# The last row block of three stages kept in SBUF for the next stage's operand

## The chip, the cores and the metric

The kernel runs on one core of a Trainium2 chip. The metric is the time of one execution in microseconds of the device; a kernel is run several times, and its time is the median. The engines of the core work side by side, each through its own row of instructions in a fixed order: TensorE (PE) multiplies, VectorE (DVE) and ScalarE (ACT) work on tiles in the on-chip memory (SBUF), GpSimd (POOL) and SyncE (SP) issue most of the transfers (DMAs) between SBUF and the memory of the chip. An instruction starts when the one ahead of it on its engine has, and when what it reads and the room that it writes are free.

## What is computed

One layer of a decoder, for 512 tokens of 2048 values in float32. Two branches (a spatial gating unit and an attention without softmax) give `y_a` and `y_b`; what matters here is what follows them:

```python
merged = sigmoid(g_a) * (y_a @ w_up_a) + sigmoid(g_b) * (y_b @ w_up_b)
x = x + merged @ w_o                                    # x1
h = rmsnorm(x, ffn_norm_g)
hid = h @ w_ffn_in
gate, up = hid[..., :FFN_HIDDEN], hid[..., FFN_HIDDEN:]
x = x + (silu(gate) * up) @ w_ffn_out                   # x2
ple = p @ w_ple
x = x + sigmoid(rmsnorm(x, ple_norm_g) @ w_ple_gate) * ple
```

## The kernel before

**Layout.** Activations are kept transposed: a block is 128 partitions by 1024 columns of float32, 512 KB, and holds 256 of the 2048 rows of x, of the merged rows or of x1 and x2 for all 512 tokens. So each of these has KU = 8 blocks, numbered 0 to 7. A product in float32 is made of products of shortened numbers: an operand is split into a high part (ScalarE, line 287 for activations and 367 for weights) and a low part (VectorE, lines 288 and 364), and TensorE adds high by high (L297), high by low weight (L299) and low by high (L298).

**Products.** A unit is the share that one row block of activations has in a pair of output blocks. It is taken plainly ("P": 12 products of 512 columns, L297 to L299) or by a scheme with seven products of half blocks in place of eight ("S", L703), which needs sums and differences of quarter blocks of the operand (L535) and of the weights (L383; some are added by GpSimd's transfers, L371). An S unit in the first output rows of a stage can still be run plainly: `HALF = 1, 1, 1, 1, 2, 2, 2, 2` and `FFN_UNTIL = 1, 1, 2, 2, 2, 2, 2, 2` say up to which output row each of the eight operands is used so. So an operand of kind S is made in two steps: first the plain parts, and later, before the first S product that needs them, the sums and differences. Both steps start from the raw block, which is loaded once for each (L526, by SP; `fetch` and `fetch_second`). At the gate the kinds are `GATE = "SSSSSSPP"`: the last two operands are plain and have one step.

**Two arenas in SBUF.** `parts` holds the operands; `wholes` has 13312 columns, room for 13 raw blocks of 1024, for everything else that is loaded or summed: raw blocks for operands, raw weights, output rows. A load waits until the block that it is given has been left by its last reader.

**What sets the order.** The program text is written once, in Python, and there is no order by hand. `tick()` runs once for each group of products. It moves on up to AHEAD = 3 of the operands in `builds`, the second steps in `seconds`, the weights planned ahead, and the functions in a waiting list: `after(n, fn)` runs `fn` n ticks later. An operand asks for room first; when `ready` says that its raw block is stored, `fetch` issues the load, and the split follows WAIT = 2 ticks later (`due`). So a change in when room is taken or given back moves later instructions on all engines.

**The stages around the change.** (1) For each of the 8 blocks j of merged rows, the two up-projections are multiplied by their gates and added (L1403); two ticks later `store` (L1376) writes the block to the chip's memory (L1377), marks it in `there` and gives its room back. The operands `ms` of w_o load it again. (2) w_o: each output is added onto the rows of x; the sum, x1, is written out (L1423), its squares go into the norm, and its room is given back. The operands `fs` of w_ffn_in load it again and scale it by the norm's gain (L530). (3) w_ffn_in, the hidden rows, which are written out and loaded back, and w_ffn_out in three chunks of the hidden rows; the first two chunks are added onto x1 in the chip's memory, the third onto a loaded x1, which gives x2 (L1481). Its operands `gs` at the gate load it again. The weights' loads (L340 plain; L342 and L350 for S) are on SP's queue as well, between all of these.

In all three places the block in question, j = 7, is the last that the stage before makes, and the first step of its operand is the last to be made.

Of the kernel before, what the change touches and what calls it, by code (L numbers as in the profile page):

```python
# [23 lines left out]
KU = D // (2 * P)  # L24
# [47 lines left out]
def hybrid_layer(  # L72
# [117 lines left out]
    clock = [0]  # L190
# [13 lines left out]
    def after(n, fn):  # L204
        heapq.heappush(waiting, (clock[0] + n, next(names), fn))
# [247 lines left out]
    class Form(Staged):  # L453
# [8 lines left out]

        def fetch(self):
            self.block, self.there, self.due = self.src(), True, clock[0] + WAIT
            self.sizes = self.sizes[:-1]

        def arrived(self):
# [905 lines left out]
            lambda size=1024: load(spill[n, j], size), lambda: (n, j) in there, gain, far=True,  # L1373
            **how)

    def store(n, j, block):  # L1376
        nc.sync.dma_start(out=spill[n, j], in_=block.f())  # L1377
        there.add((n, j))
        give(block)

    ms = [spilled_form("S", "mix", j) for j in range(KU)]
    build(ms)
    for j in range(KU):
        for b in "ab":
            s = load(gate_spill[b, j], 1024, "low")
            g = s.f()

            def gate(g=g):
                scaled(g, row1)
                nc.scalar.activation(g, g, AF.Sigmoid)  # L1390

            after(3, gate)
            pr = pair([ys[b, i] for i in range(4)], last=j == KU - 1, j=j,
                      until=(b == "b",) * 4)
            if pr.n["S"]:
                nc.vector.tensor_tensor(out=g, in0=g, in1=pr.o, op=ALU.mult)
            else:
                for h, ps in zip((g[:, :T], g[:, T:]), pr.ends()):
                    nc.vector.tensor_tensor(out=h, in0=h, in1=ps, op=ALU.mult)
            if b == "a":  # L1400
                part[j] = s
            else:
                nc.vector.tensor_tensor(out=g, in0=g, in1=part[j].f(), op=ALU.add)  # L1403
                give(part.pop(j))
                after(2, lambda j=j, s=s: store("mix", j, s))
        if not j:
            ple_operands()
        elif j < 6:
            ple_pair(j + 2)
            if j == 5:  # L1410
                ple_done()
# [5 lines left out]
    for j in range(KU):  # L1417
        h = load(xT[j])
        if j == 1:
            build(fs)  # L1420
        pr = pair(ms, last=j == KU - 1, j=j, until=HALF, doubled=7)
        pr.onto(h.f())
        nc.sync.dma_start(out=spill["x1", j], in_=h.f())  # L1423
        there.add(("x1", j))
        norm2.add(h)
        give(h)

# [33 lines left out]
    for c, units in enumerate(hs):  # L1463
# [3 lines left out]
        for j in range(KU):  # L1467
# [13 lines left out]
            nc.sync.dma_start(out=spill["x2", j], in_=h.f())  # L1481
            there.add(("x2", j))
            norm3.add(h)
            give(h)


    for j in range(KU):
# [130 lines left out]
```

## Time and profile before

| | |
|---|---|
| three runs | 2648.46, 2652.16, 2646.56 us; median 2648.46 |
| the profiled execution | 2647.41 us, of which the span of the profile is 2645.7 |
| granted clock of TensorE | 1.00 |
| busy: ScalarE, GpSimd | 54%, 17% of the span |
| read and written | 514.88 MB and 51.38 MB, 214 GB/s over the span |
| SP's queue (q1) | 444.70 MB, 51.3% of the time of 16 DMA engines |
| POOL's queue (q0) | 121.14 MB, 28.6% |

All times inside the execution are in us from the start of the span, and of one profiled execution; the span leaves out what lies around it, 1.7 us. A row of the timeline gives start, length, engine, line, operation, what it writes and reads, the shape, and how many like it follow one another; in brackets stands the idle time of the engine ahead of it with what ended it. SPq and DVEq are the parts of an engine that issue transfers and wait for them. TensorE overlaps its products, so the length of one is more than the distance between two.

### The profile page before, as it was taken

To read this page: it belongs to the slowest core of one execution; us is meant where nothing else is said; L and a number is where in the kernel's file an instruction comes from. 1 tells how busy PE (TensorE), PEld (TensorE's weight loads), DVE (VectorE), ACT (ScalarE), POOL (GpSimd) and SP (SyncE) were. 2 spreads that over 40 slices of the span, in tenths; PEclk is the share of its full clock that TensorE was granted. 3 is DMA by queue.
4 is the path that set the end of the run, shared out by engine and by line. 5 is a ranking of instruction groups with operands and counts; after the bars stand their busy time and mean duration, and the time that the engine had idled before them with its cause. 6 is when DMAs were issued, how large, how long until landed. Compare 5 with 4: busy or idle time off the path is not lost.

```text
span 2645.7 us, 43096 instructions
## 1 busy us (share of the span) xinstructions
PE 2631.0 (99%) x15454; PEld 2310.3 (87%) x15454; DVE 2300.3 (87%) x3953; ACT 1431.3 (54%) x2279; POOL 455.7 (17%) x573
## 2 busy tenths in 40 slices
PE   9999999999999999999999999999999999999999
PEld 7888888889998998888888888888888888889888
DVE  8687878787888779999888888888889989989898
ACT  7756565665555445465444444444445445455543
POOL 0222222232220001102111111111110211211010
PEclk9999999999999999999999999999999999999999
DMA  6777777777777879989988888788877989988884
GB/s 207 186 195 172 193 171 187 178 188 191 178 192 243 253 242 285 255 262 239 233 199 206 199 203 205 195 211 198 206 183 225 256 222 271 228 237 262 246 268 136
DMA packets 294533, 569.10 MB, mean 215 GB/s; under 512 B 26800, under 2 KB 137648, under 8 KB 294320
## 3 DMA queue, kind: packets, MB, share of 16 engines
q1 hardware_dynamic: 230240, 444.70, 51.3%
q0 software_dynamic: 63792, 121.14, 28.6%
q8 instruction: 121, 1.98, 0.3%
q14 instruction: 92, 0.75, 0.1%
q10 hardware_dynamic: 288, 0.52, 0.1%
HBM read 514.88 MB, written 51.38 MB: 214 GB/s over the span
## 4 chain that ended last, share of the span: by engine, by line
PE 91%; DVE 5%; DMA 2%; issue 1%; ACT 1%; SPq 0%; POOL 0%; DVEq 0%; ACTq 0%
PE ps L703 57%; PE ps L299 8%; PE ps L298 8%; PE ps L297 8%; PE small L703 6%; DVE wlo L364 1%; DVE parts L288 1%; DVE wholes L535 1%; PE small L1131 1%; PE small L1183 1%; PE small L1057 1%; DMA wholes<-hid 1%; DVE wholes L383 0%; PE small L1242 0%; ACT whi L367 0%
## 5 line engine op out<-in xcount | busy, mean ns | idle before, releaser
L703 PE MATMUL ps<-parts,whi 128*128 128x512 f32 x4390 | 1469.9, 398 | 0.1
L367 ACT ACTIVATE whi<-wholes 128x512 fp32r<-128x512 f32 (+2 forms) x948 | 883.5, 946 | 717.8 <-DVE wholes L383 324.3
L364 DVE TENSOR_TENSOR wlo<-wholes,whi 128x512 fp32r<-128x512 f32 (+2 forms) x948 | 993.3, 1083 | 40.4 <-ACT whi L367 39.9
L703 PEld LDWEIGHTS ps<-parts,wlo 128*128 128x128 f32 x4390 | 823.7, 188 | 188.0 <-DVE wlo L364 3.4
L703 PE MATMUL ps<-parts,wlo 128*128 128x256 f32 x4390 | 869.3, 279 | 1.4 <-DVE wlo L364 1.4
L703 PEld LDWEIGHTS ps<-parts,whi 128*128 128x128 f32 x4390 | 708.0, 189 | 9.5 <-issue 1.9
L299 PE MATMUL ps<-parts,wlo 128*128 128x256 f32 (+1 forms) x1706 | 550.8, 324 | 1.6 <-DVE wlo L364 1.6
L298 PE MATMUL ps<-parts,whi 128*128 128x256 f32 (+1 forms) x1706 | 551.3, 324 | 0.9 <-DVE parts L288 0.9
L297 PE MATMUL ps<-parts,whi 128*128 128x256 f32 (+1 forms) x1696 | 545.0, 323 | 2.6 <-ACT parts L287 1.8
L383 DVE TENSOR_TENSOR wholes<-wholes 128x256 f32<-128x256 f32 x848 | 357.5, 422 | 19.0 <-DMA wholes<-w_up_b 2.3
L298 PEld LDWEIGHTS ps<-parts,whi 128*128 128x128 f32 x1706 | 322.9, 189 | 34.1 <-DVE parts L288 2.7
L762 DVE TENSOR_TENSOR out<-out,ps 128x256 f32<-128x256 f32 x525 | 216.6, 416 | 151.8 <-ACT out L759 151.4
L299 PEld LDWEIGHTS ps<-parts,wlo 128*128 128x128 f32 x1706 | 323.3, 189 | 27.2 <-DVE wlo L364 2.3
L297 PEld LDWEIGHTS ps<-parts,whi 128*128 128x128 f32 x1696 | 320.6, 190 | 28.5 <-ACT parts L287 2.9
L371 POOL DMA_DIRECT2D wholes<-w_ffn_in x169 | 147.6, 873 | 703.5 <-DVE wholes L383 216.0
L371 POOL DMA_DIRECT2D wholes<-w_in x132 | 117.7, 896 | 551.2 <-DMA wholes<-w_in 125.0
L703 PE MATMUL small<-parts,whi 128*128 128x512 f32 x480 | 190.2, 396 | 0.0
L288 DVE TENSOR_TENSOR parts<-wholes,parts 128x1024 fp32r<-128x1024 f32 (+3 forms) x145 | 128.7, 902 | 10.5 <-ACT parts L287 10.5
L287 ACT ACTIVATE parts<-wholes 128x256 fp32r<-128x256 f32 (+3 forms) x145 | 112.0, 796 | 46.4 <-DVE wholes L535 35.0
L759 ACT ACTIVATE out<-ps 128x256 f32<-128x256 f32 x279 | 104.3, 385 | 57.3 <-PE ps L703 53.6
L1441 ACT ACTIVATE out<-out 128x512 f32<-128x512 f32 x44 | 27.9, 633 | 162.4 <-DVE out L1440 162.4
L371 POOL DMA_DIRECT2D wholes<-w_ffn_out x64 | 56.0, 875 | 337.2 <-DVE wlo L364 83.8
(139 smaller groups left out, 1867.0 us busy)
## 6 DMA issues: line engine op xcount, KB each, us to landing
wholes<-w_ffn_in SPq DMA_DIRECT2D x169, 384.0 KB, 5.6
wholes<-w_in SPq DMA_DIRECT2D x132, 384.0 KB, 5.1
wholes<-w_ffn_in SPq DMA_DIRECT2D x169, 256.0 KB, 4.9
wholes<-w_ffn_in POOLq DMA_DIRECT2D x169, 256.0 KB, 5.3
wholes<-w_in SPq DMA_DIRECT2D x132, 256.0 KB, 4.3
wholes<-w_in POOLq DMA_DIRECT2D x132, 256.0 KB, 5.1
wholes<-w_ffn_out SPq DMA_DIRECT2D x64, 384.0 KB, 6.1
wholes<-x SPq DMA_DIRECT2D x46, 512.0 KB, 5.8
```

The costliest lines, as they stand in the source:

```text
L287: return (nc.scalar.activation(hi, src, AF.Copy), nc.vector.tensor_tensor(out=lo, in0=src, in1=hi.bitcast(F32), op=ALU.subtract))
L288: nc.vector.tensor_tensor(out=lo, in0=src, in1=hi.bitcast(F32), op=ALU.subtract))
L297: nc.tensor.matmul(ps, sh, mh, start=start, stop=False)
L298: nc.tensor.matmul(ps, sh, ml, start=False, stop=False)
L299: return nc.tensor.matmul(ps, sl, mh, start=False, stop=stop)
L364: in_turn(nc.vector.tensor_tensor(out=self.lo[:, blocks], in0=r, in1=h.bitcast(F32), op=ALU.subtract))
L367: in_turn(nc.scalar.activation(h, r, AF.Copy))
L371: nc.gpsimd.dma_start(out=raw[:, 3:5], in_=self.src[:, 1:3], accum_op=ALU.add)
L383: in_turn(nc.vector.tensor_tensor(out=o, in0=x, in1=y, op=ALU.add))
L703: m = nc.tensor.matmul(out, l, r, start=first and k == 0, stop=last and k == 1)
L759: in_turn(nc.scalar.activation(out, x, AF.Copy, scale=scale))
L762: in_turn(nc.vector.tensor_tensor(out=out, in0=x, in1=y, op=op))
```

## The change

A new method `keep` takes the place of the first load for one operand. The block that the stage before has just summed isn't given back to the arena but handed to the operand as its raw block, there at once (`due` is the present tick, not two later). The operand's list of room to ask for loses its last entry, as after a load. It is used for j = 7 of the merged rows, of x1 and of x2. The stores stay. Besides, the last merged block is stored, and so handed over, one tick after its sum and not two. The second step of an S operand still loads the block.

```diff
@@ -462,6 +462,11 @@
 
         def fetch(self):
             self.block, self.there, self.due = self.src(), True, clock[0] + WAIT
+            self.sizes = self.sizes[:-1]
+
+        def keep(self, block):
+
+            self.block, self.there, self.due = block, True, clock[0]
             self.sizes = self.sizes[:-1]
 
         def arrived(self):
@@ -1373,10 +1378,13 @@
             lambda size=1024: load(spill[n, j], size), lambda: (n, j) in there, gain, far=True,
             **how)
 
-    def store(n, j, block):
+    def store(n, j, block, form=None):
         nc.sync.dma_start(out=spill[n, j], in_=block.f())
         there.add((n, j))
-        give(block)
+        if form:
+            form.keep(block)
+        else:
+            give(block)
 
     ms = [spilled_form("S", "mix", j) for j in range(KU)]
     build(ms)
@@ -1402,7 +1410,8 @@
             else:
                 nc.vector.tensor_tensor(out=g, in0=g, in1=part[j].f(), op=ALU.add)
                 give(part.pop(j))
-                after(2, lambda j=j, s=s: store("mix", j, s))
+                after(2 - (j == KU - 1), lambda j=j, s=s: store(
+                    "mix", j, s, ms[j] if j == KU - 1 else None))
         if not j:
             ple_operands()
         elif j < 6:
@@ -1423,7 +1432,10 @@
         nc.sync.dma_start(out=spill["x1", j], in_=h.f())
         there.add(("x1", j))
         norm2.add(h)
-        give(h)
+        if j == KU - 1:
+            fs[j].keep(h)
+        else:
+            give(h)
 
 
 
@@ -1481,7 +1493,10 @@
             nc.sync.dma_start(out=spill["x2", j], in_=h.f())
             there.add(("x2", j))
             norm3.add(h)
-            give(h)
+            if j == KU - 1:
+                gs[j].keep(h)
+            else:
+                give(h)
 
 
     for j in range(KU):
```

In the changed file the lines move: 526 becomes 531, 535 becomes 540, 1377 becomes 1382, 1423 becomes 1432. SP issues 1217 transfers in place of 1220. The number of instructions on the other engines is the same; their order differs in a few places, of which three follow. A name with a number, as mix_8278, is one block in the chip's memory: mix_8277 to mix_8284 are the merged blocks 0 to 7, the x tiles 8285 to 8292 are the blocks 0 to 7 of x1.

VectorE where w_o starts, from the low part of two pieces of weights on (wlo); L535 adds quarters of a raw block for an operand, L288 makes the low part of an operand. The block of 128x4x256 is that of merged block 7. Before:

```order
L364 TENSOR_TENSOR wlo_78<-wholes,whi_77 128x1280
L364 TENSOR_TENSOR wlo_78<-wholes,whi_77 128x512
L383 TENSOR_TENSOR wholes<-wholes 128x256
L535 TENSOR_TENSOR wholes<-wholes 128x256
L383 TENSOR_TENSOR wholes<-wholes 128x256
L535 TENSOR_TENSOR wholes<-wholes 128x2x256
L535 TENSOR_TENSOR wholes<-wholes 128x256
L288 TENSOR_TENSOR parts<-wholes,parts 128x4x256
L364 TENSOR_TENSOR wlo_76<-wholes,whi_75 128x1280
L364 TENSOR_TENSOR wlo_76<-wholes,whi_75 128x512
```

Now:

```order
L364 TENSOR_TENSOR wlo_78<-wholes,whi_77 128x1280
L364 TENSOR_TENSOR wlo_78<-wholes,whi_77 128x512
L288 TENSOR_TENSOR parts<-wholes,parts 128x4x256
L383 TENSOR_TENSOR wholes<-wholes 128x256
L540 TENSOR_TENSOR wholes<-wholes 128x256
L383 TENSOR_TENSOR wholes<-wholes 128x256
L540 TENSOR_TENSOR wholes<-wholes 128x2x256
L540 TENSOR_TENSOR wholes<-wholes 128x256
L364 TENSOR_TENSOR wlo_76<-wholes,whi_75 128x1280
L364 TENSOR_TENSOR wlo_76<-wholes,whi_75 128x512
```

The low part of block 7 has moved from behind the five additions to ahead of them; the rest keeps its order.

SP at the same place, from the store of merged block 7 (L1377) on; mix_8278 to mix_8281 are the second loads of blocks 1 to 4, xT a block of x onto which an output of w_o is added. Before:

```order
L1377 DMA mix_8284<-wholes 128x1024
L340 DMA wholes<-w_o 128x1024
L526 DMA wholes<-mix_8278 128x1024
L526 DMA wholes<-mix_8284 128x1024
L342 DMA wholes<-w_o 128x2x256
L350 DMA wholes<-w_o 128x768
L526 DMA wholes<-mix_8279 128x1024
L526 DMA wholes<-xT 128x1024
L526 DMA wholes<-mix_8281 128x1024
L342 DMA wholes<-w_o 128x2x256
L350 DMA wholes<-w_o 128x768
L526 DMA wholes<-mix_8280 128x1024
```

Now:

```order
L531 DMA wholes<-mix_8278 128x1024
L1382 DMA mix_8284<-wholes 128x1024
L340 DMA wholes<-w_o 128x1024
L531 DMA wholes<-mix_8279 128x1024
L531 DMA wholes<-mix_8280 128x1024
L342 DMA wholes<-w_o 128x2x256
L350 DMA wholes<-w_o 128x768
L531 DMA wholes<-mix_8281 128x1024
L342 DMA wholes<-w_o 128x2x256
L350 DMA wholes<-w_o 128x768
L531 DMA wholes<-xT 128x1024
```

The first load of block 7 is gone; the second load of block 1 stands ahead of the store, and those of blocks 2 and 3 ahead of the weights that were between them.

SP where w_ffn_in starts, from the second loads of the x1 blocks 3 and 4 on; each pair of L342 and L350 is one piece of weights, x_790_8292 is block 7. Before:

```order
L526 DMA wholes<-x_786_8288 128x1024
L526 DMA wholes<-x_787_8289 128x1024
L342 DMA wholes<-w_ffn_in 128x2x256
L350 DMA wholes<-w_ffn_in 128x768
L526 DMA wholes<-x_788_8290 128x1024
L526 DMA wholes<-x_789_8291 128x1024
L526 DMA wholes<-x_790_8292 128x1024
L342 DMA wholes<-w_ffn_in 128x2x256
L350 DMA wholes<-w_ffn_in 128x768
```

Now:

```order
L531 DMA wholes<-x_787_8289 128x1024
L531 DMA wholes<-x_788_8290 128x1024
L531 DMA wholes<-x_789_8291 128x1024
L342 DMA wholes<-w_ffn_in 128x2x256
L350 DMA wholes<-w_ffn_in 128x768
L342 DMA wholes<-w_ffn_in 128x2x256
L350 DMA wholes<-w_ffn_in 128x768
L531 DMA wholes<-x_790_8292 128x1024
L342 DMA wholes<-w_ffn_in 128x2x256
```

The second load of block 7, the last of three in a row before, now follows two pairs of weights.

## The prediction

> **What bounds the kernel now.** I read the page first, then the busy time by stretch, then what TensorE waited for, then the chain and the rows of the place that the chain names.
>
> ```profile
> PE 2631.0 (99%) x15454; PEld 2310.3 (87%) x15454; DVE 2300.3 (87%) x3953; ACT 1431.3 (54%) x2279; POOL 455.7 (17%) x573
> ```
>
> TensorE is busy for 2631.0 of the span's 2645.7 us, so all that it does not do is 14.7 us, and nothing in the change touches the number of its products. The change can only take or give waits of TensorE at the three handovers that it edits: merged rows to w_o (about 990 to 1050 us), x1 to w_ffn_in (about 1160 to 1210), x2 to the gate (about 2475 to 2530). Columns: stretch, length, then busy time (and count) of PE, PEld, DVE, ACT and POOL, granted clock, share of the DMA engines, GB/s.
>
> ```profile
> 1000.00:1050.00 50.00, 48.82 (x267) 41.61 (x266) 45.49 (x76) 24.40 (x31) 5.55 (x7) 1.00 0.94 293
> 1050.00:1200.00 150.00, 150.00 (x830) 129.83 (x829) 144.45 (x255) 93.99 (x132) 21.29 (x24) 1.00 0.89 257
> 1200.00:1250.00 50.00, 49.92 (x284) 42.83 (x283) 49.48 (x91) 25.72 (x38) 9.62 (x11) 1.00 0.89 237
> 2480.00:2530.00 50.00, 49.53 (x254) 41.79 (x254) 44.05 (x76) 30.70 (x47) 5.58 (x6) 1.00 0.91 277
> ```
>
> At the first handover TensorE lacks 1.18 us of 50; from 1050 to 1200, with the whole x1 handover in it, it lacks nothing; at the gate 0.47 of 50. VectorE is nearly full in all of them (45.49 and 49.48 of 50), and the DMA engines are at 0.94 in the first. Who TensorE waited for, over the whole run (total, times, longest) and then from 1000 to 1250 us:
>
> ```profile
> PE ps L703 <- DVE wlo L364: 1.4, 3, 0.6
> ...
> PE ps L297 <- ACT parts L287: 0.5, 1, 0.5
> PE ps L298 <- DVE parts L288: 0.4, 1, 0.4
> PE ps L703 <- DVE wlo L364: 0.3, 1, 0.3
> ```
>
> L287 and L288 write the high and the low part of a merged block into the operand; L364 splits weights. So at the first handover TensorE waits for operands, and the chain of waits says which:
>
> ```profile
> 999.77 1.23 DVE wholes L1403
> 1001.01 4.63 DMA mix<-wholes
> 1005.71 4.95 DMA wholes<-mix
> 1010.68 1.07 ACT parts L287
> 1011.77 1.14 DVE parts L288
> ```
>
> The last block of merged rows is summed on VectorE until 1001.00, stored until 1005.64, loaded back until 1010.66, and only then split. TensorE's own rows (start, length) show what this costs it:
>
> ```profile
> 1012.26 0.39 PE L297 MATMUL ps<-parts,whi 128*128 128x512 f32 x1
> 1013.05 0.50 PE L298 MATMUL ps<-parts,whi 128*128 128x512 f32 x1 [0.40 <-DVE parts L288]
> 1013.39 0.39 PE L299 MATMUL ps<-parts,wlo 128*128 128x512 f32 x1
> ...
> 1021.43 0.28 PE L297 MATMUL ps<-parts,whi 128*128 128x256 f32 x1
> 1021.62 0.38 PE L298 MATMUL ps<-parts,whi 128*128 128x256 f32 x1
> 1021.85 0.28 PE L299 MATMUL ps<-parts,wlo 128*128 128x256 f32 x1
> ...
> 1024.35 0.40 PE L298 MATMUL ps<-parts,whi 128*128 128x512 f32 x1
> 1025.26 0.62 PE L297 MATMUL ps<-parts,whi 128*128 128x256 f32 x3 [0.51 <-ACT parts L287]
> 1025.72 0.40 PE L299 MATMUL ps<-parts,wlo 128*128 128x512 f32 x1
> ```
>
> A 512-wide product starts 0.23 us after the one before it, a 256-wide one 0.12 us. At 1013.05 the start comes 0.79 after the last one and the next 0.34 after that: 0.56 and 0.11 too late, 0.67 in all. At 1021.62 it is 0.07 and 0.11, so 0.18. At 1025.26 it is 0.68, and the three that follow take 0.46 in place of 0.36: 0.78. Together **1.63 us**. The product at 1012.26 is the first of the last unit (eight units of 12 products at 0.227 us from 993.2), and the one at 1013.05 the first that needs that unit's low part: exactly the block that went through memory.
>
> **What the change removes, adds and moves.** Three loads of 512 KB go, one at each handover; the stores stay, since the second preparation step and the later sums still read them. The kept block stays taken until its first split: one of the 13 blocks of 1024 columns that the arena of whole blocks holds.
>
> Merged rows. The split of the last block now needs only the sum at 1001.00. ScalarE's rows there, then VectorE's (whi and wlo are the high and low part of weights, parts the operands, wholes the raw blocks; L383 adds weights, L535 adds blocks):
>
> ```profile
> 1004.13 1.79 ACT L367 ACTIVATE whi<-wholes 128x1280 fp32r<-128x1280 f32 x2 [2.02 <-PE ps L298]
> 1010.68 1.06 ACT L287 ACTIVATE parts<-wholes 128x1024 fp32r<-128x1024 f32 x1 [4.76 <-DMA wholes<-mix]
> 1011.64 1.78 ACT L367 ACTIVATE whi<-wholes 128x1280 fp32r<-128x1280 f32 x2
> ...
> 1002.37 1.22 DVE L288 TENSOR_TENSOR parts<-wholes,parts 128x1024 fp32r<-128x1024 f32 x1
> ...
> 1005.44 2.09 DVE L364 TENSOR_TENSOR wlo<-wholes,whi 128x1280 fp32r<-128x1280 f32 x2
> ...
> 1009.51 0.42 DVE L535 TENSOR_TENSOR wholes<-wholes 128x256 f32<-128x256 f32 x1 [1.52 <-DMA wholes<-mix]
> 1011.77 1.23 DVE L288 TENSOR_TENSOR parts<-wholes,parts 128x1024 fp32r<-128x1024 f32 x1 [0.43 <-ACT parts L287]
> 1012.93 2.09 DVE L364 TENSOR_TENSOR wlo<-wholes,whi 128x1280 fp32r<-128x1280 f32 x2
> 1025.24 1.23 DVE L288 TENSOR_TENSOR parts<-wholes,parts 128x1024 fp32r<-128x1024 f32 x1 [1.12 <-ACT parts L287]
> ```
>
> ScalarE keeps the split (L287) at its place in the row, behind the weights of 1004.13, so it runs from 5.92 to 6.98 (us after 1000) in place of 10.68. VectorE's part moves up, as its rows under the change show: the 128x4x256 split has gone from behind five additions to ahead of them: it starts at 7.5 and ends at 8.7, where TensorE needs it at 12.5. The spare time is 3.8 us, so the 0.67 goes whole. It also stands in an idle stretch now: VectorE was idle for 1.52 before 1009.51 and 0.43 before 1011.77, and the weights behind it (L364 at 1012.93) wait for a slot that TensorE leaves after six units, at 1009.5, and then for ScalarE's high part (1.28 us, the share of the 1280 columns in the 1.79 for two). They can start at about 11.0, 1.9 us sooner, and the three operand splits behind them (L288) with them, less the 0.3 us that the new order puts ahead of one of them. The two later waits of TensorE are for these splits; it will ask for them only 0.67 and 0.85 sooner. So 0.18 and 0.78 go too, if the raw blocks of the second step are there. These are loads on SP's queue. In SP's rows under the change the second loads of blocks 1, 2 and 3 (mix_8278 to 8280), whose splits the first S products need, are the ones to watch. Blocks 2 and 3 now come ahead of the weights and of xT and block 4. Block 1's load moves ahead of the store, and waits there for its own place in the arena:
>
> ```profile
> 997.61 0.33 SPq L340 DMA_DIRECT2D wholes<-w_o  x1
> ...
> 1002.53 3.51 SPq L526 DMA_DIRECT2D wholes<-mix  x2
> ```
>
> It was issued at 1002.53 (the second issue of that row is the load that goes, 1005.71) and VectorE had it at 1009.51. No row shows how long it will wait now: at best it issues at 997.9, right behind the load before it; at worst when VectorE's last split of a merged block before that (1002.37 with 1.22) leaves its block, 1003.6. So its use moves by -1.5 (no more than the idle time there) to +1.1 us; even +1.1 leaves the chain 0.8 ahead, against 0.18 to 0.85 needed. I take 0. The store behind it is read only by the second load of the same block, many rows later. The tick by which the store is sooner is worth nothing: it was issued at 1001.01, 0.01 us after the sum.
>
> What stays late next: the wait of 0.3 us for weights at 1046. It ends a stretch in which VectorE is nearly full and which TensorE's own results start; the order in it keeps the same set of instructions ahead of those weights. TensorE and this stretch both come 1.6 us sooner, and the wait stays.
>
> x1. TensorE has 150.00 of 150.00 us busy, so the load that goes was hidden by the plain products that come first: gain 0. What the change can do there is below, as the slower rival. x2. The last two units are plain at the gate, and no wait of TensorE names their load; its only wait to 2530 is for weights (in the 1.4, 3 of the row above). The new order puts an operand split of 768 columns (0.9 us by the 1.23 for 1024) ahead of VectorE's sums of the outputs, and a weight split of 1.28 ahead of ScalarE's sigmoid: later outputs, sooner operands. I take 0, between -0.47, TensorE's whole idle time there, and +0.9, the split if it delayed a weight split that TensorE waits for.
>
> A rule of the Trainium skill speaks against all this. DMA: Bandwidth & Descriptors, section Anatomy of one DMA, fits a DMA as 2.0 us plus the bytes over 436 GB/s; for 512 KB that is 3.2 us, 6.4 for store and load, where this trace has 4.63 and 4.95. By that fit of the Trainium skill the block would have been back at 1007.4 and split by 1009.7, ahead of TensorE's need, and the first term would be 0 instead of 0.67; the trace, with the DMA engines at 0.94, decides. The same page of the Trainium skill (Rules for kernel authors) says that a transfer issued early and waited for late hides its fixed cost; by the rows above that holds here for x1, and for the merged rows it fails by 0.67 us.
>
> **The sum**: -0.67 - 0.18 - 0.78 = -1.63 us. The profiled execution took 2647.41 us (span 2645.7 and 1.7 around it), which gives 2645.8. It lies 1.05 below the median of the three runs, 2648.46; the same sum from the median gives **2646.8**, which I forecast.
>
> **The rivals.** (a) *Only the first wait goes.* The second loads land no sooner, VectorE stays full from 1012 to 1024, and the waits at 1021.62 and 1025.26 slide to be as long as before: -0.67, 2647.8. For it: DMA share 0.94, and VectorE was released by a load at 1009.51. Against it: blocks 2 and 3 are asked for ahead of two loads of weights.
> (b) *It frees more.* The three waits for weights at L703 (1.4 us in all: merged rows, hidden rows, gate) are ends of full VectorE stretches; the moved orders shorten some. If all go: -3.0, 2645.4. Nothing but the moved order speaks for it.
> (c) *A load takes the place of the wait, at x1.* In SP's rows of the x1 handover the second load of the last block (x_790_8292) was the third of three loads in a row, and now stands behind two pairs of weights. The rows of before (the issues, the second pair, the first use, and all loads of x1 with their median time to landing):
>
> ```profile
> 1179.80 5.07 SPq L526 DMA_DIRECT2D wholes<-x  x3
> ...
> 1189.88 0.38 SPq L342 DMA_DIRECT2D wholes<-w_ffn_in  x1
> 1190.31 0.46 SPq L350 DMA_DIRECT2D wholes<-w_ffn_in  x1
> ...
> 1197.57 1.32 ACT L530 ACTIVATE wholes<-wholes,gcol 128x512 f32<-128x512 f32 x2
> ...
> wholes<-x SPq DMA_DIRECT2D x46, 512.0 KB, 5.8
> ```
>
> It was issued by 1184.87; the second pair stood at 1189.88 to 1190.77, so it now comes at about 1190.8 and lands 5.8 us later, at 1196.6; its first use was at 1197.57, so 1.0 us is left. From a landing after that on, ScalarE and VectorE stand in their rows, the weights behind them, and VectorE has 0.5 us idle in the next 50 to catch up. No row gives TensorE's own reserve there. It names no wait for these splits, so it is above 0; I put it at 5, one stand of SP in the row above, an estimate. To be slower by 5.3 us the load would have to come 1.0 + 5 + 5.3 = 11.3 us later than I reckon, as if SP stood for two more such rows (5.07 each): 2653.8. Small slips of this kind at any of the three places give 2649 to 2651.
> (d) *The change does nothing here*, because the reload is not what holds the split: 2648.5. Against it, SP's list has 1217 issues in place of 1220, and the chain row by row.
>
> **How the numbers follow.** About 0.2%, 5.3 us, is what a measurement of this kernel can tell from no change. Chances: forecast 0.50, (a) 0.14, (b) 0.14, (c) 0.12, of which 0.06 beyond 5.3 us, (d) 0.10. All but the ends of (b) and (c) lie within 0.2% of 2648.46. The median of three runs that themselves differ by 5.6 us can add 2 us either way, so I give faster by over 0.2% 0.08, within 0.2% 0.84, slower 0.08. The range is 2642.5 to 2651.5: (b) less 2 us and a little, and (c) small.
>
> **What would show it.** Right: the chain no longer has mix<-wholes and wholes<-mix; the last L287 of the first handover starts near 1006; no TensorE wait for L287 or L288 between 1000 and 1030; TensorE reaches the next stages 1.6 us sooner; the 0.3 at 1046 remains. Wrong: a wait of VectorE for wholes<-mix near 1009 or 1018 (a); TensorE waits for L364 or L288 from 1180 to 1225 or from 2500 to 2530 (c); a span that moves by more than 4 us, which nothing above can give.

## The result and the profile after

| | before | changed |
|---|---|---|
| median of 20 runs | 2652.24 us (2646.56 to 2659.77) | 2645.31 us (2642.95 to 2650.23) |
| profiled execution | 2647.41, span 2645.7 | 2643.73, span 2641.9 |
| ratio | | 0.9974, 95% interval 0.9968 to 0.9981 |

The changed kernel is faster by about 6.9 us (5.0 to 8.5 by the interval). The forecast time, 2646.8, is 1.5 us above the median, but the forecast gain was 1.6 us, so **most of the gain is not in the forecast's sum**. The forecast put a change within 0.2% at 0.84 and a gain of more at 0.08; the ratio is 0.26% below 1. The three runs that the forecast started from had a median of 2648.46; all twenty have 2652.24, so the profiled execution of before, at 2647.41, was one of its quickest.

The page of the changed kernel (busy time, then the chain that ended last, by engine), its stretches at the three edited handovers, and what TensorE waited for from 980 us on (total, times, longest):

```profile
PE 2628.6 (99%) x15454; PEld 2311.0 (87%) x15454; DVE 2300.7 (87%) x3953; ACT 1430.9 (54%) x2279; POOL 459.8 (17%) x573
...
PE 95%; DVE 3%; ACT 1%; issue 1%; DMA 1%; POOL 0%; DVEq 0%; ACTq 0%; SPq 0%
```

```profile
1000.00:1050.00 50.00, 49.84 (x276) 43.16 (x275) 48.29 (x79) 27.54 (x35) 6.95 (x8) 1.00 0.95 294
1050.00:1200.00 150.00, 150.00 (x831) 129.87 (x830) 142.76 (x253) 90.88 (x128) 20.37 (x23) 1.00 0.88 251
1200.00:1250.00 50.00, 49.83 (x286) 43.34 (x285) 49.55 (x91) 26.89 (x41) 9.60 (x11) 1.00 0.91 237
2480.00:2530.00 50.00, 50.00 (x266) 42.66 (x265) 43.87 (x75) 30.86 (x45) 4.41 (x5) 1.00 0.88 266
```

```profile
PE ps L708 <- DVE out L813: 0.3, 2, 0.2
PE ps L297 <- ACT parts L287: 0.3, 1, 0.3
```

L703 of before is L708 here. From 1000 to 1050 TensorE now lacks 0.16 us of 50 where it lacked 1.18, at the gate nothing where it lacked 0.47. After 980 us the view names no wait for weights (L364) any more, and 0.6 us of waits in all. Now the rows of the merged handover, SP's first, then ScalarE's and VectorE's; TensorE reaches the stage 1.0 us later than in the profile of before, so 1.0 is to be taken off for a comparison:

```profile
1000.98 0.33 SPq L531 DMA_DIRECT2D wholes<-mix  x1
1002.08 0.33 SPq L1382 DMA_DIRECT2D mix<-wholes  x1
...
1004.69 0.89 SPq L531 DMA_DIRECT2D wholes<-mix  x2
...
1005.19 1.79 ACT L367 ACTIVATE whi<-wholes 128x1280 fp32r<-128x1280 f32 x2 [2.17 <-issue]
1006.89 1.05 ACT L287 ACTIVATE parts<-wholes 128x1024 fp32r<-128x1024 f32 x1
...
1006.50 2.09 DVE L364 TENSOR_TENSOR wlo<-wholes,whi 128x1280 fp32r<-128x1280 f32 x2
1008.52 1.22 DVE L288 TENSOR_TENSOR parts<-wholes,parts 128x1024 fp32r<-128x1024 f32 x1
...
1011.94 2.10 DVE L364 TENSOR_TENSOR wlo<-wholes,whi 128x1280 fp32r<-128x1280 f32 x2
```

Block 1's second load (1000.98) is ahead of the store of block 7 (1002.08), those of blocks 2 and 3 follow at 1004.69, and there is no reload of block 7. Its high part (L287) follows the weights at 1006.89, its low part (L288) the weights at 1008.52, with no idle time ahead of either, and the next weights start at 1011.94.

**A yardstick for the experiments.** One execution differs from the next by several us in places that no kernel here touches: from TensorE's 3700th product to its 4100th, ahead of everything edited, the profiles below take 59.7 to 64.1 us. So the runs are compared by stretches: the time between the starts of two of TensorE's 15454 products, numbered in order of start, the same numbers in every kernel. Each of four stretches holds one place that the change moves: *merged*, products 6150 to 6450 (about 1010 to 1064 us); *x1*, 7100 to 7400 (1181 to 1236); *w_ffn_out*, 12900 to 14300 (2203 to 2442, the second and third chunk); *gate*, 14300 to 14900 (2442 to 2547). The table has one profile of each run, so each stretch is of one execution, in us; the ratio is that of the timed runs to the kernel before on the same chip, and stands in the text below with its 95% interval in brackets. M, X1, X2 say which blocks 7 are kept, T that w_ffn_out has the changed kernel's order of rows.

| run | has | merged | x1 | w_ffn_out | gate | ratio |
|---|---|---|---|---|---|---|
| the kernel before | - | 53.55 | 55.10 | 238.53 | 105.30 |  |
| a1, the same again | - | 54.09 | 56.01 | 239.71 | 106.08 | 0.9997 |
| a2 | M | 51.76 | 55.19 | 238.24 | 107.96 | 0.9980 |
| a3 | X1, T | 54.10 | 55.11 | 236.63 | 106.32 | 0.9994 |
| a4 | X2 | 55.74 | 56.32 | 237.66 | 105.81 | 1.0003 |
| b1 | T | 53.89 | 55.88 | 235.71 | 106.17 | 0.9997 |
| b2 | M, X1, X2 | 51.76 | 55.34 | 240.37 | 104.76 | 0.9987 |
| b3 | - | 53.46 | 55.19 | 237.35 | 105.90 | 1.0004 |
| b4 | block 6, T | 53.07 | 55.89 | 235.72 | 105.38 | 0.9992 |
| c2 | M, T | 52.49 | 55.19 | 236.29 | 105.77 | 0.9984 |
| c3 | M, X1, T | 52.10 | 54.86 | 236.13 | 105.70 | 0.9977 |
| d1 | M, X2, T | 51.82 | 55.14 | 235.71 | 104.55 | 0.9977 |
| the changed kernel | M, X1, X2, T | 51.78 | 54.84 | 235.99 | 104.57 | 0.9974 |
| c1, the same again | M, X1, X2, T | 51.83 | 54.84 | 235.98 | 104.51 | 0.9977 |

### The profile page after: what moved, and what is told of

It reads as the page before. It is cut to its first block, busy times and chain, and to the rows that moved or that the text cites. A ratio compares the mean times of both kernels' runs of the same rounds, so it can differ in the third digit from the quotient of the medians.

```text
span 2641.9 us, 43106 instructions
## 1 busy us (share of the span) xinstructions
PE 2628.6 (99%) x15454; PEld 2311.0 (87%) x15454; DVE 2300.7 (87%) x3953; ACT 1430.9 (54%) x2279; POOL 459.8 (17%) x573
## 4 chain that ended last, share of the span: by engine, by line
PE 95%; DVE 3%; ACT 1%; issue 1%; DMA 1%; POOL 0%; DVEq 0%; ACTq 0%; SPq 0%
PE ps L708 57%; PE ps L299 9%; PE ps L298 9%; PE ps L297 9%; PE small L708 6%; DVE wlo L364 1%; PE small L1188 1%; PE small L1136 1%; PE small L1062 1%; DVE wholes L540 1%; DVE parts L288 1%; PE small L297 0%; PE small L299 0%; PE small L298 0%; PE small L1247 0%
## 5 line engine op out<-in xcount | busy, mean ns | idle before, releaser
L708 PE MATMUL ps<-parts,whi 128*128 128x512 f32 x4390 | 1469.3, 398 | 0.3 <-DVE out L813 0.3
L367 ACT ACTIVATE whi<-wholes 128x512 fp32r<-128x512 f32 (+2 forms) x948 | 884.2, 946 | 736.3 <-DVE wholes L383 321.7
L364 DVE TENSOR_TENSOR wlo<-wholes,whi 128x512 fp32r<-128x512 f32 (+2 forms) x948 | 994.3, 1086 | 40.7 <-ACT whi L367 39.8
L708 PEld LDWEIGHTS ps<-parts,wlo 128*128 128x128 f32 x4390 | 824.2, 188 | 186.0 <-issue 1.9
L708 PE MATMUL ps<-parts,wlo 128*128 128x256 f32 x4390 | 868.1, 279 | 0.0
L708 PEld LDWEIGHTS ps<-parts,whi 128*128 128x128 f32 x4390 | 707.3, 189 | 8.7 <-issue 2.5
L708 PE MATMUL small<-parts,whi 128*128 128x512 f32 x480 | 190.1, 396 | 0.0
L288 DVE TENSOR_TENSOR parts<-wholes,parts 128x1024 fp32r<-128x1024 f32 (+3 forms) x145 | 129.5, 908 | 6.0 <-ACT parts L287 5.7
L287 ACT ACTIVATE parts<-wholes 128x1024 fp32r<-128x1024 f32 (+3 forms) x145 | 112.0, 795 | 33.7 <-DVE wholes L540 28.2
```

The lines of the kernel that those rows point to most:

```text
L287: return (nc.scalar.activation(hi, src, AF.Copy), nc.vector.tensor_tensor(out=lo, in0=src, in1=hi.bitcast(F32), op=ALU.subtract))
L288: nc.vector.tensor_tensor(out=lo, in0=src, in1=hi.bitcast(F32), op=ALU.subtract))
L364: in_turn(nc.vector.tensor_tensor(out=self.lo[:, blocks], in0=r, in1=h.bitcast(F32), op=ALU.subtract))
L367: in_turn(nc.scalar.activation(h, r, AF.Copy))
L708: m = nc.tensor.matmul(out, l, r, start=first and k == 0, stop=last and k == 1)
```

## The experiments

The theories at the outset: (A) each edit frees the waits that its own moved rows held; (B) the merged handover is the whole effect, and the waits that the changed profile lacks after 2200 us were accidents of one execution. Each run has 10 or 11 timed executions, beside 15 to 33 of the kernel before on the same chip.

**The kernel before again, and each edit alone.** In the diffs the left side is the kernel before; they show the edited lines alone, without the method `keep` and the argument `form` of `store`, which are as in the change.

> The kernel before, unchanged: the ratio is 1. It is run for its profile and for the clock of each run. Two readings of the 1.2 us of waits that the profile of the changed kernel lacks at the second chunk of w_ffn_out (2234) and of the 1.3 at the third (2379 and 2410) and of the 0.7 at the gate (2528): if they belong to the program (theory A), this second profile has waits of TensorE for L364 or L288 at the same four products, 0.4 to 0.9 us each; if they are accidents of one execution (theory B), at most one or two of the four come back at the same product. If the granted clock makes the spread of the runs, the runs' spans go with it: 0.001 of clock is 2.6 us.

Ratio 0.9997 (0.9988 to 1.0006). Of the four waits, those at 2234, 2410 and 2528 come back at the same products (2239, 2413 and 2532 in this later execution), the one at 2379 doesn't. The granted clock explains a part of the spread at most: of 107 runs of the kernel before beside the experiments, the 40 at 1.000 took 2651.4 us in the mean, the 63 at 0.999 took 2652.1 and the four at 0.998 took 2656.9, but those at 1.000 alone reach from 2648.3 to 2656.1. The chain of waits of this second profile at the merged handover, and the product that waits:

```profile
1002.25 4.64 DMA mix<-wholes
1006.96 5.32 DMA wholes<-mix
1012.30 1.07 ACT parts L287
1013.39 1.14 DVE parts L288
```

```profile
1014.67 0.50 PE L298 MATMUL ps<-parts,whi 128*128 128x512 f32 x1 [0.76 <-DVE parts L288]
```

The same chain as in the first profile, with a load of 5.32 us for 4.95, and a wait of 0.76 for 0.4.

```diff
-                after(2, lambda j=j, s=s: store("mix", j, s))
+                after(2 - (j == KU - 1), lambda j=j, s=s: store(
+                    "mix", j, s, ms[j] if j == KU - 1 else None))
```

> Only the merged block is kept and stored a tick sooner; x1 and x2 are given back and loaded again. Theory A (each edit frees the waits that its own moved rows held): -1.7 us, ratio 0.9994, and the waits at 2234, 2379, 2410 and 2528 are still there. Theory B (the merged handover is the whole effect, and later waits are accidents): the whole of the change, ratio 0.997 to 0.998. In both the waits at 1013, 1021 and 1025 are gone.

Ratio 0.9980 (0.9971 to 0.9989): by the time alone this is the edge of what theory B gave, and more than theory A did. The stretch of the merged rows falls to 51.76, against 53.55 to 55.74 in the profiles that load the block in before's order. The waits at 2235 and 2380 stay (0.64 and 0.83 us), so B's second half does not hold; but that at 2410 has shrunk to 0.26 by the starts, and that at 2528 is gone, where A had both stay. The execution with the longest stretch (x2 alone kept) shows that more than the forecast chain hangs on the reload:

```profile
1007.23 4.91 DMA wholes<-mix
...
1017.67 7.96 DMA wholes<-mix
1025.66 2.04 DVE wholes L540 x5
1027.73 1.06 ACT parts L287
```

```profile
1028.84 0.62 PE L297 MATMUL ps<-parts,whi 128*128 128x256 f32 x3 [2.61 <-ACT parts L287]
```

After the reload of block 7 a second-step load stands in the chain, issued only at 1017.67, 7.96 us long: TensorE waits 2.61 us at 1028.84, where the first profile had 0.51. In the changed order the second loads of blocks 2 and 3 come sooner (the two of 1004.69 above), and the products there start 0.15 us late in the seven profiles with the block kept.

```diff
-        give(h)
+        if j == KU - 1:
+            fs[j].keep(h)
+        else:
+            give(h)
```

> Only block 7 of x1 is kept. Theory A: the rows of w_ffn_out move with this edit, so the waits at 2234, 2379 and 2410 go (-2.5 us, ratio 0.9990), and those at 1013 to 1025 stay. Theory B: no measurable gain, ratio 1.000 within 0.0003, and waits of about a us in all somewhere between 2200 and 2420. The rival of the prediction, a late second load of block 7 at w_ffn_in, would show as a wait of TensorE between 1190 and 1225 and a ratio over 1.

Ratio 0.9994 (0.9985 to 1.0002). The waits at 2234, 2379 and 2410 are gone, though nothing was edited there, and w_ffn_out takes 236.63 us against 237.66 to 239.71 in before, a1, a2 and a4. Between 2200 and 2420 one wait of 0.7 us is left, at 2249, which no other profile has. The late second load of block 7, the forecast's rival, does not show in TensorE's waits.

```diff
-            give(h)
+            if j == KU - 1:
+                gs[j].keep(h)
+            else:
+                give(h)
```

> Only block 7 of x2 is kept. Theory A: the wait of 0.7 us at 2528 goes, the others stay: -0.6 us, ratio 0.9998. Theory B: 1.000. The forecast had 0, between -0.47 and +0.9.

Ratio 1.0003 (0.9994 to 1.0012): by the time nothing to be seen, and the gate's stretch (105.81) does not separate yet. The wait at 2528 is gone, but two others stand nearby, by the starts 0.5 us at 2526 and 1.7 at 2554.

**Why x1's edit reaches w_ffn_out.** Nothing in the rows of x1 lies beside w_ffn_out; about 1000 us are between them. What lasts is the arena's record of when each free place was given back, by which a load "old" picks the place left longest ago. When the Python program that sets the order is written out tick by tick (a tick is a step of this program, not a time), the free room is the same in both kernels from tick 442 to 768, and only this record differs; from 769 on the places differ, and at 901 one more operand finds room a tick sooner. The record can be set without keeping any block:

```diff
         if m == KH - 1:
             build(hs[0])
+            for at, n, ago in ((4, 10, 5), (14, 10, 9), (24, 6, 6)):
+                wholes.given[at : at + n] = wholes.turns - ago
```

> The kernel before with all three loads, and only the record of which free places in SBUF were left longest ago set, at the start of w_ffn_out, to what it is when x1's last block is kept. That gives w_ffn_out and the gate the order of rows that they have with x1 kept, and leaves everything before it as it was. Theory A (the part of the gain at w_ffn_out is this order and not the load): the waits of about 0.8 us at 2234 to 2239 and of 0.6 to 0.9 at 2410 to 2414 are gone, -1.5 us, ratio 0.9994; those at the merged rows (53.6 to 55.7 us for the stretch from product 6150 to 6450) stay. Theory C (x1's share is its load): both waits are still there, ratio 1.000.

The stretch of w_ffn_out is 235.71 us, as short as with any block kept, and the waits at 2234 and 2410 are gone; merged rows and x1 are as before. The median is 1.5 us below that of before; the ratio, 0.9997 (0.9989 to 1.0006), cannot tell 1.5 us from nothing. The rows that moved are VectorE's. Before's order (a1) and this one, with the product of a1 that waits:

```profile
2234.75 0.95 DVE L288 TENSOR_TENSOR parts<-wholes,parts 128x768 fp32r<-128x768 f32 x1
...
2236.96 0.95 DVE L288 TENSOR_TENSOR parts<-wholes,parts 128x768 fp32r<-128x768 f32 x1
2237.83 1.48 DVE L364 TENSOR_TENSOR wlo<-wholes,whi 128x1280 fp32r<-128x1280 f32 x1
```

```profile
2239.36 0.50 PE L703 MATMUL ps<-parts,wlo 128*128 128x256 f32 x2 [0.65 <-DVE wlo L364]
```

```profile
2230.62 0.95 DVE L288 TENSOR_TENSOR parts<-wholes,parts 128x768 fp32r<-128x768 f32 x1
...
2232.50 1.48 DVE L364 TENSOR_TENSOR wlo<-wholes,whi 128x1280 fp32r<-128x1280 f32 x1
```

The low part of the weights (L364, 128x1280) starts 5.33 us sooner in the second. TensorE's 13050th product is 2.75 us sooner there (2230.06 against 2232.81), so the weights come 2.6 us ahead of where they stood, and the wait of 0.65 is gone: one of the operand splits ahead of them was made earlier. The other way round, in the changed kernel:

```diff
+            for at, n, ago in ((4, 10, 12), (14, 10, 11), (24, 6, 10)):
+                wholes.given[at : at + n] = wholes.turns - ago
```

> The changed kernel with all three blocks kept, and only that record set back to what it is in the kernel before: w_ffn_out runs in the order of before. Theory A: the waits at 2234 and 2410 come back, so of the change's 0.9974 about 0.9980 is left. Theory C: as the changed kernel, 0.9974.

```profile
2238.14 0.51 PE L708 MATMUL ps<-parts,wlo 128*128 128x256 f32 x2 [0.64 <-DVE wlo L364]
...
2414.64 0.39 PE L299 MATMUL ps<-parts,wlo 128*128 128x256 f32 x1 [0.93 <-DVE wlo L364]
```

Both waits are back (0.64 and 0.93), w_ffn_out takes 240.37 us, and the ratio is 0.9987 (0.9978 to 0.9996) where 0.9980 was expected: with all three blocks kept, a part of the gain hangs on the record of places, by the ratio half, but the interval leaves room for much less. By the stretches of both runs, x1's share at w_ffn_out is an order of rows, not a load.

**Is it the reload, at the merged rows?**

```diff
-                after(2, lambda j=j, s=s: store("mix", j, s))
+                after(2 - (j == KU - 1), lambda j=j, s=s: store("mix", j, s))
```

> Only the store of the last merged block comes a tick sooner; the block is given back and loaded again. SP's list has the second loads of blocks 1 and 2 moved up as in the changed kernel, with the load of block 7 among them. Theory A (the store and load of block 7 hold the split): the waits for L287 and L288 between 1010 and 1030 stay, stretch 6150 to 6450 as before (53.6 to 55.7 us), ratio 1.000. Rival (the moved second loads give the gain at the merged rows): the stretch is near 51.8, ratio 0.998.

```profile
1014.31 0.73 PE L297 MATMUL ps<-parts,whi 128*128 128x512 f32 x2 [0.67 <-ACT parts L287]
...
1026.23 0.62 PE L297 MATMUL ps<-parts,whi 128*128 128x256 f32 x3 [0.66 <-ACT parts L287]
```

Ratio 1.0004 (0.9996 to 1.0013), stretch 53.46, and both waits for L287 are there, 0.67 and 0.66 us. The second load of block 1 stands ahead of the store and that of block 2 close behind it, as in the changed kernel, but block 7's reload after them, and block 3's load is not moved up: while the reload stays, these moved loads bring no more than the executions differ by. (With the block kept, the program gives the same rows in the same order on every engine with one tick or two, so the tick is worth nothing there either.)

```diff
-                after(2, lambda j=j, s=s: store("mix", j, s))
+                after(2, lambda j=j, s=s: store(
+                    "mix", j, s, ms[j] if j == KU - 2 else None))
```

> Merged block 6 is kept in place of block 7; x1 and x2 are not kept. One load of 512 KB goes at the same place, but not that of the last block. Its record of places happens to give w_ffn_out the order of x1 kept, too. Theory A: the wait at 1013 to 1015 for block 7's low part is still there, stretch 6150 to 6450 at 53.6 to 55.7; the time is that of the run with that order alone (0.9994). Rival (one transfer less relieves the queue and the memory at this place): the stretch falls to 52 to 53 and the ratio to 0.998.

This missed its band on both sides: the stretch is 53.07, just under before's, and the wait at 1012 for block 7 is there but small (0.28 by the starts); others, for weights and for results, stand in its place:

```profile
1044.21 0.50 PE L708 MATMUL ps<-parts,wlo 128*128 128x256 f32 x2 [0.30 <-DVE wlo L364]
...
1057.02 0.50 PE L708 MATMUL ps<-parts,whi 128*128 128x512 f32 x1 [0.21 <-DVE out L767]
```

The ratio, 0.9992 (0.9983 to 1.0001), holds the order of w_ffn_out as well (235.72). One transfer less at this place gives 0.4 us of the stretch against b3, 1.2 against the mean of those in before's order; the last block kept gives 2.3. A part by relief of the queue is not excluded.

**The sum, and what is left for x1's and x2's loads.**

> The changed kernel again. If the parts so far are the whole (merged rows -2.5 us as the mean of the profiles against 51.8, order of w_ffn_out -2.6, x1's load -0.5, x2 nothing), the ratio is 0.9974 to 0.9980, and a second profile has the same short stretches: 51.8 us from product 6150 to 6450, 36.9 from 14050 to 14300, no wait of half a us at 2234 or 2410.

0.9977 (0.9968 to 0.9987), and the stretches come back within 0.1 us: 51.83, 54.84, 235.98 and 104.51 against 51.78, 54.84, 235.99 and 104.57.

> The merged block is kept, x1's and x2's are loaded again, and the record of places is set at the start of w_ffn_out to what x1 kept would leave. Theory A: nearly all of the change, 0.9976 to 0.9982, 0 to 0.6 us short of the run of the changed kernel beside it, by the wait near 1185 for x1's last block that comes in some executions. If x1's or x2's load were worth more by itself, it is 0.9985 or above.

0.9984 (0.9975 to 0.9992), a little short of what was expected, and not told apart from the run beside it.

> Merged and x1 blocks kept, x2's loaded again. Theory A: as the changed kernel beside it within 0.0003, since at the gate no stretch of the profiles with x2 kept differs from those without by more than they differ among themselves. If keeping x2 gains or costs, it shows here against the changed kernel by more than 0.0004.

0.9977 (0.9968 to 0.9986), as the changed kernel beside it. By the time alone x2's load would be worth nothing. The gate's stretches say otherwise: with x2's block loaded again they are 105.30 to 107.96 us, with it kept 104.51 to 105.81; among those with the same order T, 105.38 to 106.32 in five that load it and 104.51 and 104.57 in the two of the changed kernel. In the longest (merged alone kept), TensorE's longest wait after 980 us and the chain that leads to it read:

```profile
PE small L974 <- DVE diag L972: 1.6, 1, 1.6
```

```profile
2476.56 6.13 DMA x<-wholes
2482.70 5.72 DMA wholes<-x
2488.45 0.73 ACT parts L535
2489.21 0.65 DVE parts L635
2489.88 0.74 DVE parts L635
2490.62 0.21 DVE diag L972
```

Block 7 of x2 goes out (6.13), comes back (5.72), and is split for its plain operand (L535 on ScalarE, L635 on VectorE). No wait of TensorE is for this operand. But behind the split, in VectorE's row, stands `diag` (L972), a small step of the norm that TensorE spreads over the partitions (L974), and TensorE waited 1.6 us for that. In the changed kernel the split is not held:

```profile
2483.51 1.41 DVE L635 SCALAR_TENSOR_TENSOR parts<-wholes,gcol,parts 128x512 fp32r<-128x512 f32 x2
2484.84 0.48 DVE L972 TENSOR_SCALAR diag<-ident,cols 128x128 f32<-128x128 f32 x2
```

Two more profiles with the reload have this wait behind the same store and load, 1.4 and 1.1 us (b1 and b3); none with the block kept has over 0.3. In the other six with the reload the wait for `diag` is 0.5 us at most, but each has one near 2530 for weights, of 0.2 to 1.1 us, which no profile with the block kept has. In c3, which differs from the changed kernel in x2's block alone, the chain of that wait leads back to the same place (L367 is the high part of weights):

```profile
2473.66 4.68 DMA x<-wholes
2478.36 5.87 DMA wholes<-x
...
2485.79 5.42 DMA wholes<-x
...
2525.52 0.64 ACT whi L367
2526.20 0.73 PE ps L708 x2
```

Block 7 goes out (4.68) and comes back (5.87); the load at 2485.79 is issued when VectorE has done its split, and what follows is late up to the weights at 2525.52, for which TensorE waits 0.46. The profile of a3 has the same chain to its wait of 1.07; that of the kernel before has another.

Two readings were left, whether x2's load costs this time or not, and the last run was made for them. It keeps M and X2 and sets the record of places as in b1:

> Merged and x2 blocks kept, only x1's loaded again, and the record of places set as x1 kept would leave it; from w_ffn_out on it has the rows of the changed kernel. What is open: in 3 of 9 profiles with x2's block loaded again TensorE waited 1.2 to 1.7 us near 2490 for VectorE's diag, behind store, load and split of that block; in 4 with it kept 0.4 at most. Theory (x2's load costs about 1 us, now and then): products 14300 to 14900 take 104.5 to 105.8 us as in those four, against 105.3 to 108.0 with the load, and the ratio is 0.9976 to 0.9980, below the 0.9984 of the run without x2 kept. Rival (those waits have nothing to do with x2's load): a stretch anywhere up to 108, ratio as 0.9984. For x1: products 7100 to 7400 take 55.1 to 56.3, against 54.8 to 55.3 with x1 kept.

The gate takes 104.55 us, within 0.1 of the changed kernel's, and the ratio is 0.9977 (0.9968 to 0.9986): x2's theory holds by the stretch, and the ratio, below the 0.9984 of c2, agrees with it without deciding it. x1 takes 55.14, hardly more than with the block kept.

## Why the prediction was right and where it failed

The means of the stretches, with and without each part: merged 54.27 (five profiles that load it in before's order) against 51.93 (seven kept), **2.3 us**; x1 55.55 (nine) against 55.00 (five), **0.6**; w_ffn_out 238.64 (six in before's order) against 236.02 (eight in the changed one), **2.6**; gate 106.06 (nine) against 104.84 (five), **1.2**. The sum is 6.7 us, where the timed runs gave 6.9.

How the gain is shared out is less sure than the sum. By the medians of the timed runs, each beside the kernel before on its chip, M alone gives 3.5 us (its ratio says 5.3, 2.9 to 7.7), T alone 1.5, M and T together 4.7, the changed kernel 6.2 and 6.9. So the merged rows are probably worth more than the 2.3 of these few profiles and w_ffn_out less than 2.6, and which of the two is the larger part stays open.

- *The bound, and "the change can only take or give waits of TensorE at the three handovers that it edits".* The number of products stayed, and each of the four parts shows as waits of TensorE that went. But the 14.7 us of idle time were no bound: of the 3.8 us between the two first spans, 2.4 went from TensorE's busy time (2631.0 to 2628.6), because the view counts a product of 512 columns as busy for 0.39 us where the next can start 0.23 us after it, and so hides the first 0.16 us of a wait (the product at 1013.05 was 0.56 late by the starts, 0.40 in the view). **"At the three handovers that it edits" is the step that failed.** 2.6 us by the stretches, 1.5 by the medians of b1, went at w_ffn_out, 1000 us behind the nearest edit ahead of it, since a block given back later changes which places later loads take. The order of rows showed these moves before the run; they were not priced. Rival (b) came nearest: of its three waits for weights at L703 those at 2234 and 2528 went. It had a chance of 0.14 and 1.4 us for three places, and that its time, 2645.4, is the measured one is luck, as it too starts from the median of three runs.
- *Merged rows, -0.67 - 0.18 - 0.78.* The mechanism was right row by row: with the 1.0 us taken off, L287 starts at 5.9 (forecast 5.92), L288 at 7.5 (7.5), the weights behind it at 10.9 (11.0); block 1's second load issues at 1000.0, between 997.9 and 1003.6, and VectorE doesn't wait for it. At 1046 the same product is late again (0.32 by the starts, 0.15 in the view), but behind an output of VectorE (L813), not the weights that the forecast named. Between the two first profiles the stretch shrank by 1.77, near the 1.63. But the term was worked out from the execution of before that lost nearly least there. The mean is 2.3, and the timed runs of M alone say 3.5: the size was off, not the mechanism. Rival (a) falls, as the waits at 1021 and 1025 went too.
- *x1, 0.* Nearly: 0.6 us in the mean, by a wait of 0.7 to 1.1 us that four of the nine profiles with the load have, the first not among them, and none of the five with the block kept. In the second profile of before (SP's issues, ScalarE, TensorE):

```profile
1166.69 4.46 SPq L526 DMA_DIRECT2D wholes<-x  x4
...
1176.48 0.80 SPq L526 DMA_DIRECT2D wholes<-x  x2
...
1182.83 1.34 ACT L530 ACTIVATE wholes<-wholes,gcol 128x512 f32<-128x512 f32 x2 [0.83 <-DMA wholes<-x]
```

```profile
1185.16 0.85 PE L297 MATMUL ps<-parts,whi 128*128 128x256 f32 x4 [0.81 <-ACT parts L287]
```

  After a row of four loads, of which block 7's is one, the next two were issued at 1176.48, and ScalarE waited 0.83, TensorE 0.81 us for the first of them, which took 6.32 us. Keeping the block removes the load and moves later ones up; which of the two ends the wait, no run separates. The three profiles with the merged block kept and x1 loaded don't have it, and are 0.3 us longer than the changed kernel (55.14 to 55.19 against 54.84). "TensorE has 150.00 of 150.00" was true of one execution.
- *Rival (c), the late second load of block 7.* It did come late, later than worked out, and cost ScalarE something:

```profile
1193.45 0.33 SPq L531 DMA_DIRECT2D wholes<-x  x1
...
1199.78 0.72 ACT L535 ACTIVATE wholes<-wholes,gcol 128x512 f32<-128x512 f32 x1 [0.78 <-DMA wholes<-x]
```

  Issued at 1193.45 (forecast 1190.8), it held ScalarE for 0.78 us at 1199.78; no wait of TensorE for an operand followed in that stretch, so TensorE's reserve, which the forecast put at 5 as an estimate, was at least larger than this delay.
- *x2, 0 between -0.47 and +0.9.* The step that failed is "no wait of TensorE names their load". The waits name `diag` and weights, whose rows stand behind the reload's split in the chain; in the first profile `diag` came just in time. -1.2 in the mean lies outside the ends given.
- *The rule of the Trainium skill* (DMA: Bandwidth & Descriptors, Anatomy of one DMA) would have given 3.2 us a transfer, an estimate by that page, and 0 for the first term. In four profiles with the load in before's order the store of block 7 took 4.04 to 4.80 us and its load 4.91 to 5.82, so the measurement decides against it here. The section's fit is for the path of GpSimd's queue, and these transfers are on SP's, so it was no fair rule for them to begin with.
- *The numbers.* The range (2642.5 to 2651.5) held the time; 2646.8 came near it by two errors against each other: the gain was too small by 5 us, and the median of three runs that it was taken from was 3.8 us below that of twenty. The 0.08 for "faster by over 0.2%" was too low: every term was read from the one profiled execution, near the fast end. The forecast's own sign of being wrong, "a span that moves by more than 4 us, which nothing above can give", is not met by the two first spans (3.8) but by the medians (6.9).

Not settled: how much of the merged rows' 2.3 us is relief of the queue rather than the block's own way through memory (the run with block 6 kept leaves up to 1.2 us open), how the gain is divided between the merged rows and w_ffn_out, and x1's and x2's shares in time, which are shown by stretches and chains but are smaller than the intervals of the timed runs. None of the runs beats the changed kernel; c3 and d1 are as fast within the interval. The waits that the view names after 980 us add up to 0.6 and 1.9 us in the changed kernel's two profiles.

## What to carry to other kernels

A store and reload at a stage's end is priced from several executions, not one: where the load lands about when it is needed, one profile may show a wait of 0.5 us, and another 2.6. Look not only at who reads the reloaded block but at what stands behind its split in the same engine's row. And where a planner hands out places, an edit that gives room back later reorders stages far behind it: compare the order over the whole program, and price each place where an engine that is waited for has moved. Stretches of single profiles show where a gain lies, but their sizes are to be held against timed runs of each part.

## What the runs showed of the hardware

Transfers of the same size and queue vary widely: the loads of 512 KB that SP issues at L526 took 3.3 to 10.1 us in the first profile, 5.8 in the median, and the same second-step load took 7.96 us in one execution and 6.03 and 6.17 in two others. The spread between executions is made of such lateness in part: in one (c2), at a stage that no edit touches, TensorE's waits between 630 and 650 us are these:

```profile
PE small L1247 <- ACT wholes L1085: 2.6, 1, 2.6
```

Behind it stood a load of w_in of 5.78 us (3.33 in the first profile, which has no such wait); a sum by GpSimd's transfer and a power on GpSimd came between it and ScalarE's step.
